# Three more projection units multiplied as eight plain half products, the last attention heads in six steps, the retention gates in a pipeline, and the final norm on three engines

## The chip, the cores and the metric

One core of a Trainium2 chip. The number compared is the device time of one execution in microseconds (us), the median of the runs. A difference of 0.3% (8 us) is about what a measurement of this kernel can tell from no change.

## The reference

Two layers on x of 512 tokens by 2048 (S by D), all in fp32, post-normed: x becomes LayerNorm(2^0.5 · x + branch(x)).

```python
# layer one, "FoX": 16 heads of 128
q, k, v, gate, f = split(x @ fox_w_in)              # 4 x 2048 columns + 16
q, k = rms_norm per head; c = cumsum(log_sigmoid(f + b))
s = q @ k.T * 128**-0.5 + c[query] - c[key]         # causal
y = (softmax(s) @ v) * silu(gate);  branch = y @ fox_w_out
# layer two, retention: 8 heads, q and k of 256, v and gate of 512
q, k, v, gate = split(x @ ret_w_in);  q, k = rotary(q, k)
o = ((q @ k.T) * decay) @ v                         # causal, by chunks
y = group_norm(o) * silu(gate);  branch = y @ ret_w_out
```

## The kernel before, in words

**Products.** fp32 operands are split into a high and a low part (`w_h`, `w_l`: an ACT copy, L288, and a DVE subtraction, L289), and each product is three matmuls (high by high, low by high, high by low; L293, L294, L295). The projections are cut into *units*: 16 narrow ones (n0 to n15; 256-column matmuls; queries and keys of two attention heads or of one retention head) and 18 wide ones (w0 to w17; 512 columns; values and gates, and the two output projections, w4, w5 and w14 to w17). A unit is a 2x2 block product. A `Unit` computes it as seven half products (Strassen's scheme): besides the four input blocks it needs four sums of them (`s1` to `s4`) and sums of weights, made block by block on DVE (L494, L498). A `Plain` takes the input blocks `a11`, `a12`, `a21`, `a22` and the weights as they are, in eight half products, and no sums. Each half product is 48 matmuls in four *blocks* of twelve (wide) or two of 24 (narrow); each loads 512 KB of weights on SP's queue. Before, n0, w4 and n8 are `Plain`, the rest `Unit`s.

**Order.** A class `Order` writes out the instruction streams in program order. A *slot* is one block's matmuls; behind it go steps of waiting *tasks* (a generator's code up to its next `yield need(...)`) as far as rings of buffers are free and the running debt of DVE and ACT allows. Where a block cannot go on for want of a buffer or input (`require`), the tasks' steps are written one behind the other with no block between them: a *clump*. Engines run their streams in order. The units' order is n0, w0, n1, w1, n2, n3, w2, n4, n5, w3, n6, n7, w4, w5, half of n8, half of w6, the rest of both, then n9, w7, n10, w8, ..., n15, w13, w14 to w17.

**Around the change.** After each of n0 to n7 a `Pair` of heads is normed (`normed`) and attends (`head`): scores (`scores`, PE), addition of the query's decay on ACT (`c_tok`, L1031), running minimum on DVE, exponential, scaling by the reciprocal sum (ACT), transposes, product with the values (L1058), gating. The result `y`, and its negative `ny`, go by DMAs to DRAM (`y_s`, where the DMA sums them to `s1` to `s4`) and come back for w4 and w5 (`y_raw`). Then the first norm (`to_columns`) turns z into the input blocks of layer two. In layer two `attend` (rotary on DVE, `rope`; split to `qk_h` on ACT) and `retain` (product `inner` by v, group norm, gates) belong to each head. At `retain`'s end four gate tiles (`p` or `gate`) are scaled by `gn_r` (ACT, L1517), transposed (PE, L1521), and evicted as `y` and `ny` (ACT, L1528, L1529); `gate_done` behind the second frees buffer `k0`, which the next wide unit takes for its kept product (`keep`, ACT, L358). Last, w16 and w17 add into z (L1223), and `store` norms a block of 128 tokens with two DVE instructions for each 512 columns (L1609, L1610).

Of the kernel before, what the change touches and what calls it, by code (L numbers as in the profile page):

```python
# [17 lines left out]
P = 128  # L18
D = 2048
# [24 lines left out]
def blocks_of(n, *groups):  # L44

    def of(g):
# [13 lines left out]
EACH = [[(k, n, c, m) for k in (1, 2) for c in range(2) for n in range(2)] for m in range(2)]  # L60

HELD = ([(1, 0, c, m) for c in range(4) for m in range(2)] + [(1, 1, c, 0) for c in range(4)]
        + [(2, 0, c, m) for c in range(4) for m in range(2)] + [(2, 1, c, 0) for c in range(4)]
# [9 lines left out]
RINGS = dict(mmp=2, tmp=4, st=3, q=4, **{t: 1 for t in "k0 k1 k2 in0 in1 g0 g1 g2 d0 b0 b1 b2 f2 f6 f7 f8".split()})  # L73
# [156 lines left out]
def trunk(ctx: ExitStack, tc: tile.TileContext, xq, x, fb_f, columns, wf_in, narrow, wide, ln_g, ln_b, rot, decay,  # L230
          out):
    nc = tc.nc
    pool = ctx.enter_context(tc.tile_pool(name="sb", bufs=1))
# [33 lines left out]

    cols = pool.tile([P, 2 + 2 * KT], F32, name="cols")
# [31 lines left out]
    def new_form(name):  # L300
        forms[name] = [pool.tile([P, 8, 256], F32R, name=name, tag=t) for t in HOME[name]]
        ready[name] = set()
# [8 lines left out]
    class Unit:  # L311
# [3 lines left out]
        def __init__(self, w, n, sink, rows=True, u2="k0"):  # L315
            self.w, self.n, self.sink, self.rows, self.u2 = w, n, sink, rows, u2
# [25 lines left out]
        def keep(self, what, bank):  # L342
            n = self.shape[2]
            if self.wide or what == "u2":
                tag = {"p1": "k0", "p2": "k0", "p5": "k1", "u2": "k2"}[what] if self.wide else self.u2
# [67 lines left out]
        def sum_ahead(self):  # L413

            for i in range(2):
                t = pool.tile([P, 2, 2, 512], F32, name="v_sum", tag=HOME["s1"][i])
                for c in range(2):
                    self.summed["p7", 2 * i + c] = t[:, c]
# [25 lines left out]
    class Block:  # L444
# [59 lines left out]
        def split(self):  # L504
# [10 lines left out]
            if u.last and p == "p4":  # L515
                if c % 2 == 0:
                    u.wide_w = [sb8(f"w_{j}", HOME["a12" if c == 0 else "s2"][i], F32R)
                                              for i, j in enumerate("hl")]
# [55 lines left out]
    class Plain:  # L574


        def __init__(self, w, n, sink, tags, rows=True):
            self.w, self.n, self.sink, self.rows, self.tags = w, n, sink, rows, tags
# [6 lines left out]
        def run(self, order, then={}, before={}, ahead={}):  # L585

            for i, b in enumerate(order):
                same = last if i and order[i - 1][:3] == b[:3] else None
                last = PlainBlock(self, *b, same, then.get(i), before.get(i), ahead.get(i))
                o.push(last)  # L590

# [19 lines left out]
    class PlainBlock:  # L611
# [31 lines left out]
        def ready(self):  # L643
            n = self.u.shape[1]
            return ready.get(f"a{self.m + 1}{self.k}", set()).issuperset(range(n * self.c, n * self.c + n))

        def multiply(self):
# [5 lines left out]
            multiply(u, u.bank[at], forms[f"a{self.m + 1}{self.k}"], self.w, self.c, new, u.left[at] == 0)  # L653
# [11 lines left out]
    def new_quarters(m):  # L665
        for q, t in (("11", "f8"), ("12", "f9")) if m == 0 else (("21", "g0"), ("22", "g2")):
# [6 lines left out]
    def combine(rest, plain):  # L673
# [36 lines left out]
        yield need(until=lambda: plain.left[1, 0] == plain.left[1, 1] == 0)  # L710
        new_form("s3")
        for c in range(2):
# [8 lines left out]
           for f in HOME if i == 0 or f != "a21"} for i in range(3)]  # L721
# [7 lines left out]
    def give_forms(i, half, m, at, y, ny, but=()):  # L729

        for f, sign, more in GIVES[half, m] + ((("a21", 1, 0),) if (i, half, m) == (0, 0, 1) else ()):
            if f in but:
                continue
# [3 lines left out]
    def fetch_form(i, name, tags, at=0, to=8):  # L737

        step = 8 if tags[0][0] == "g" else 4
        for c in range(at, to, step):  # L740
            n = min(step, to - c)
            heads = 4 * i if i else c + n + (0 if name in ("a11", "a21", "s3") else 8)
            if i == 0 and name in ("s1", "s2", "s4"):
                heads = FH
            yield need(until=lambda: given[i > 0] >= heads and any(free[t] for t in tags))
            if c == 0:
# [19 lines left out]
    def fetch_while(i, tags):  # L766

        take = lambda *names: lambda: spawn(fetch_forms(i, names, tags), 1)
        return {"p5": take("a11", "s1"), "p6": take("s2"), "p7": take("s4", "s3"), "p4": take("a12", "a22")}
# [34 lines left out]
    def forget():  # L804
# [55 lines left out]
        fox["tok"] = pool.tile([P, ST, FH], F32, name="c_tok")  # L860
        yield need(mmp=1, pe=0.4)
        t = mmp()
        ct = by4(t)
        for s in range(ST):
            nc.tensor.transpose(ct[:, s, :FH], c[:, s * P:(s + 1) * P], ident[:FH, :FH])
        yield need(dve=0.3)
        nc.vector.tensor_scalar(fox["tok"], ct[:, :, :FH], -1.0, None, op0=ALU.mult)
        give("mmp")
# [806 lines left out]
```

## Time and profile before

| | us |
|---|---|
| median of three runs (lowest, highest) | 2608.29 (2603.34, 2611.29) |
| the profiled execution's own time | 2620.05 |
| span of its trace | 2618.3 |
| PE busy | 2372.2 (91%) |
| DVE busy | 1962.9 (75%) |
| ACT busy | 1268.9 (48%) |
| POOL busy | 216.5 (8%) |
| mean granted PE clock | 0.955 |

The span lacks 1.75 us of the execution's own time. PE's busy time counts a matmul at a lower granted clock with its longer duration, so part of the 91% is stretched work.

### The profile page before, as it was taken

The page shows a single profiled execution, that of the slowest core. Times are in us where ns is not written, and L with a number is a line of the kernel's source. Part 1 is how long each engine was busy: PE and PEld are TensorE (multiplying, and loading weights), DVE is VectorE, ACT ScalarE, POOL GpSimd, SP SyncE. Part 2 cuts the span into 40 slices and gives each one's busy share as a digit, 9 for nine tenths or more (in the row PEclk, how much of TensorE's full clock was granted, in tenths as well). Part 3 has the DMA queues.
Part 4 walks back from the last instruction along what each step waited for, and adds up shares of the span by engine and source line. Part 5 has one row for each costly group of instructions (what it writes and reads, how often), then busy time and mean ns, then how long its engine had stood idle before and what let it go on. Part 6 is the DMA issues. An engine that isn't in the chain of part 4 may idle for free.

```text
span 2618.3 us, 34343 instructions
## 1 busy us (share of the span) xinstructions
PE 2372.2 (91%) x12964; PEld 2037.6 (78%) x12964; DVE 1962.9 (75%) x2547; ACT 1268.9 (48%) x1891; POOL 216.5 (8%) x324
## 2 busy tenths in 40 slices
PE   7999999999989797998898999989998999699994
PEld 7788898897887575787787797968797887577783
DVE  4778777777765376597878688868887887678878
ACT  4445566666556443653443445444544454434431
POOL 0000200210110100000010101010101010110001
PEclk9999999999999898998999999989999999899997
DMA  5455665665654586454564747555754667578674
GB/s 203 137 177 159 194 197 159 210 192 148 199 150 139 135 288 189 162 169 140 178 205 149 221 157 200 166 162 188 206 193 142 200 176 250 148 249 261 213 247 148
DMA packets 194966, 484.80 MB, mean 185 GB/s; under 512 B 19040, under 2 KB 71392, under 8 KB 194800
## 3 DMA queue, kind: packets, MB, share of 16 engines
q1 hardware_dynamic: 161712, 404.46, 47.1%
q0 software_dynamic: 33088, 78.14, 12.5%
q8 instruction: 102, 1.67, 0.2%
q14 instruction: 64, 0.52, 0.1%
HBM read 412.76 MB, written 69.76 MB: 184 GB/s over the span
## 4 chain that ended last, share of the span: by engine, by line
PE 28%; DVE 18%; DMA 7%; ACT 4%; issue 3%; SPq 0%; ACTq 0%; DVEq 0%
PE acc L294 8%; PE acc L293 8%; PE acc L295 8%; DVE w_l L289 7%; DMA w_raw<-in_wide 5%; DVE w_q L498 3%; ACT w_h L288 2%; DVE w_raw L494 1%; PE mmp L293 1%; PE mmp L294 1%; PE mmp L295 1%; DMA ln_g<-in_ln_g 1%; DVE rope L1390 1%; DVE s L289 1%; DMA y_raw<-y_a 0%
## 5 line engine op out<-in xcount | busy, mean ns | idle before, releaser
L288 ACT ACTIVATE w_h<-w_q 128x1024 fp32r<-128x1024 f32 x384 | 405.2, 1058 | 472.3 <-DVE w_q L498 262.1
L289 DVE TENSOR_TENSOR w_l<-w_q,w_h 128x1024 fp32r<-128x1024 f32 x384 | 468.7, 1222 | 185.6 <-ACT w_h L288 180.7
L294 PE MATMUL acc<-w_l,s 128*128 128x512 f32 (+1 forms) x1536 | 567.6, 370 | 38.5 <-DVE w_l L289 38.3
L293 PE MATMUL acc<-w_h,s 128*128 128x512 f32 (+1 forms) x1536 | 569.0, 370 | 26.6 <-ACT w_h L288 16.3
L295 PE MATMUL acc<-w_h,s 128*128 128x512 f32 (+1 forms) x1536 | 562.7, 366 | 0.0
L293 PE MATMUL acc<-w_h,a 128*128 128x512 f32 (+1 forms) x1408 | 512.6, 364 | 29.2 <-DVE p L403 10.8
L288 ACT ACTIVATE w_h<-w_raw 128x1024 fp32r<-128x1024 f32 x328 | 345.2, 1056 | 385.2 <-PE acc L295 124.5
L289 DVE TENSOR_TENSOR w_l<-w_raw,w_h 128x1024 fp32r<-128x1024 f32 x328 | 400.2, 1221 | 150.9 <-ACT w_h L288 144.7
L294 PE MATMUL acc<-w_l,a 128*128 128x512 f32 (+1 forms) x1408 | 506.3, 360 | 4.0 <-DVE w_l L289 4.0
L295 PE MATMUL acc<-w_h,a 128*128 128x512 f32 (+1 forms) x1408 | 505.3, 359 | 0.0
L294 PEld LDWEIGHTS acc<-w_l,s 128*128 128x128 f32 x1536 | 297.3, 194 | 96.8 <-DVE w_l L289 53.6
L293 PEld LDWEIGHTS acc<-w_h,s 128*128 128x128 f32 x1536 | 297.5, 194 | 75.7 <-ACT w_h L288 18.9
L498 DVE TENSOR_TENSOR w_q<-w_q,w_raw 128x1024 f32<-128x1024 f32 x280 | 340.1, 1220 | 17.0 <-DMA w_raw<-in_wide 13.9
L295 PEld LDWEIGHTS acc<-w_h,s 128*128 128x128 f32 x1536 | 297.2, 194 | 45.3
L293 PEld LDWEIGHTS acc<-w_h,a 128*128 128x128 f32 x1408 | 271.2, 193 | 68.9 <-issue 13.7
L294 PEld LDWEIGHTS acc<-w_l,a 128*128 128x128 f32 x1408 | 271.5, 193 | 43.2 <-DVE w_l L289 7.5
L295 PEld LDWEIGHTS acc<-w_h,a 128*128 128x128 f32 x1408 | 270.8, 192 | 38.6
L494 DVE TENSOR_TENSOR w_raw<-w_raw 128x1024 f32<-128x1024 f32 x88 | 107.4, 1221 | 75.5 <-DMA w_raw<-in_wide 69.5
L295 PE MATMUL acc<-a,w_l 128*128 128x256 f32 x464 | 133.5, 288 | 3.0 <-DVE w_l L289 3.0
L293 PE MATMUL acc<-a,w_h 128*128 128x256 f32 x464 | 133.7, 288 | 0.5 <-ACT w_h L288 0.5
L294 PE MATMUL acc<-a,w_h 128*128 128x256 f32 x464 | 133.0, 287 | 0.0
L293 PE MATMUL acc<-s,w_h 128*128 128x256 f32 x448 | 127.3, 284 | 2.8 <-ACT p L358 2.8
(207 smaller groups left out, 3007.9 us busy)
## 6 DMA issues: line engine op xcount, KB each, us to landing
w_raw<-in_wide SPq DMA_DIRECT2D x364, 512.0 KB, 4.1
w_raw<-in_narrow SPq DMA_DIRECT2D x164, 512.0 KB, 3.9
w_q<-in_wide SPq DMA_DIRECT2D x68, 512.0 KB, 4.7
w_q<-in_narrow SPq DMA_DIRECT2D x28, 512.0 KB, 5.2
y_raw<-y_s SPq DMA_DIRECT2D x24, 512.0 KB, 6.1
y_s<-ny POOLq DMA_DIRECT2D x48, 256.0 KB, 6.7
y_s<-y POOLq DMA_DIRECT2D x40, 256.0 KB, 5.7
y_raw<-y_a SPq DMA_DIRECT2D x18, 512.0 KB, 5.9
```

Source lines behind the costliest of these rows:

```text
L288: nc.scalar.activation(h, src, AF.Copy)
L289: nc.vector.tensor_sub(l, src, f32(h))
L293: nc.tensor.matmul(ps, a[0], b[0], start=start, stop=False, skip_group_check=True)
L294: nc.tensor.matmul(ps, a[0], b[1], start=False, stop=False, skip_group_check=True)
L295: nc.tensor.matmul(ps, a[1], b[0], start=False, stop=stop, skip_group_check=True)
L494: nc.vector.tensor_add(self.t, self.t, u.lent.pop(("p3", c)))
L498: nc.vector.tensor_add(u.chain[c], u.chain[c], t)
L1390: nc.vector.tensor_mul(a, raw[j], cos[:, None, :].to_broadcast([P, 2, 512]))
```

## The change

1. Forty transposes of the identity `ident` stand at the start of PE's stream.
2. The query's decay `c_tok` and the ACT addition for it are gone, in all 16 heads; the minimum reads the scores from PSUM.
3. n7, w5 and w6 become `Plain`, so six units are (the instruction lists show 96 more 512-column and 48 more 256-column matmuls of `acc`, three half products). n7 reloads x's block 21 (`again`). w5 and w6 go by `EACH_N`, in which each block loads its own 512 KB.
4. With no sums needed in w5, `ny` and the DMAs for `s1` to `s4` of layer one go: 88 on POOL's queue. Heads 12 to 15 are split straight into `a12` and `a22`.
5. Heads 12 to 15 (`quick`) take six steps instead of eight, scale on DVE instead of ACT, have buffers that let two heads overlap, and `HELD` needs heads 14 and 15 three blocks later.
6. `to_columns` is spread over w5's later blocks, beside smaller moves of buffers.
7. `retain`'s gate loop becomes a pipeline: in one step ACT scales tile t, PE transposes t-1, and ACT evicts t-2.
8. w14 keeps its first product in `in0` and a later sum in `in1`, no longer in `k0` and `k2`.
9. The final norm: s0 and s1 together; ACT scales and shifts, DVE multiplies by the gain, POOL adds the bias; for s2 and s3 half of the columns so, half as before. All stores go on SP's queue.

In the retention unit w8 ACT's stream had the scale of the second gate tile behind a rotary split; `qk_h` by `rope` is that split, `p` by `gn_r` the scale, `w_h` the weights:

```order
L288 ACTIVATE w_h<-w_q 128x1024 x3
L288 ACTIVATE qk_h<-rope 128x1024
L288 ACTIVATE w_h<-w_q 128x1024 x3
L1517 ACTIVATE p_11439<-p_11439,gn_r 128x512
L288 ACTIVATE qk_h<-rope 128x1024
L1528 ACTIVATE y<-mmp 128x512
L1529 ACTIVATE ny<-mmp 128x512
L1517 ACTIVATE p_11439<-p_11439,gn_r 128x512
L358 ACTIVATE p_12663<-acc 128x1024
L288 ACTIVATE w_h<-w_q 128x1024
```

The changed kernel has at that place:

```order
L1650 ACTIVATE p_11352<-p_11352,gn_r 128x512
L296 ACTIVATE w_h<-w_q 128x1024
L1650 ACTIVATE p_11352<-p_11352,gn_r 128x512
L296 ACTIVATE w_h<-w_q 128x1024
L1641 ACTIVATE y<-mmp 128x512
L1642 ACTIVATE ny<-mmp 128x512
L1650 ACTIVATE gate<-gate,gn_r 128x512
L296 ACTIVATE w_h<-w_q 128x1024 x2
L366 ACTIVATE p_12565<-acc 128x1024
L296 ACTIVATE w_h<-w_q 128x1024
L366 ACTIVATE p_12586<-acc 128x1024
```

The first two scales now stand one weight split apart; the next `qk_h` by `rope` stands six rows further on.

In w4, PE's stream before has the last heads' steps in a clump: product with the values (`pT,by_head`), transposes of the probabilities (`ident,p`), of gates and of raw queries, with no weight block between:

```order
L1058 MATMUL mmp<-pT,by_head 128x128
L961 MATMUL mmp<-ident,p 128x128 x4
L1068 MATMUL mmp<-ident,by_head 128x128 x4
L961 MATMUL mmp<-ident,p 128x128 x3
L926 MATMUL mmp<-ident,qk_raw 128x128 x4
L961 MATMUL mmp<-ident,p 128x128 x3
L1058 MATMUL mmp<-pT,by_head 128x512
L1058 MATMUL mmp<-pT,by_head 128x384
L1058 MATMUL mmp<-pT,by_head 128x256
L1058 MATMUL mmp<-pT,by_head 128x128
```

The changed kernel, where a head's product with the values stands in w4 (`acc` rows are the unit's blocks):

```order
L301 MATMUL acc<-w_h,a_7708 128x512
L302 MATMUL acc<-w_l,a_7708 128x512
L303 MATMUL acc<-w_h,a_7709 128x512
L1117 MATMUL mmp<-pT,by_head 128x512
L1117 MATMUL mmp<-pT,by_head 128x384
L1117 MATMUL mmp<-pT,by_head 128x256
L1117 MATMUL mmp<-pT,by_head 128x128
L301 MATMUL acc<-w_h,a_7706 128x512
```

Such a product now has a block of twelve `acc` matmuls on either side.

At the end DVE's stream before had pairs of norm instructions behind the statistics of the last blocks:

```order
L1223 TENSOR_TENSOR z<-z,acc 128x512
L1227 BN_STATS ln_st<-z 128x6
L1609 SCALAR_TENSOR_TENSOR z<-z,ln_mv,ln_last 128x512
L1610 SCALAR_TENSOR_TENSOR z<-z,ln_r,ln_last 128x512
L1609 SCALAR_TENSOR_TENSOR z<-z,ln_mv,ln_last 128x512
```

and now has single multiplications of 1024 or 512 columns (L1728; their other parts are on ACT and POOL) among the pairs:

```order
L1749 SCALAR_TENSOR_TENSOR ln_nb<-ln_mv,ln_r 128x1
L1728 TENSOR_TENSOR z<-z,ln_last 128x1024
L1728 TENSOR_TENSOR z<-z,ln_last 128x512
L1756 SCALAR_TENSOR_TENSOR z<-z,ln_mv,ln_last 128x512
L1757 SCALAR_TENSOR_TENSOR z<-z,ln_r,ln_last 128x512
L1319 TENSOR_TENSOR z<-z,acc 128x512
L1323 BN_STATS ln_st<-z 128x6
L1728 TENSOR_TENSOR z<-z,ln_last 128x512
L1336 BN_AGGR ln_mv<-ln_st 128x2
```

The core of the diff:

```diff
+EACH_N = [[(k, n, c, m) for k in (1, 2) for n in range(2) for c in range(4)] for m in range(2)]
 
 HELD = ([(1, 0, c, m) for c in range(4) for m in range(2)] + [(1, 1, c, 0) for c in range(4)]
-        + [(2, 0, c, m) for c in range(4) for m in range(2)] + [(2, 1, c, 0) for c in range(4)]
+        + [(2, n, c, m) for c in range(4) for n, m in ((0, 0), (0, 1), (1, 0))]
         + [(k, 1, c, 1) for k in (1, 2) for c in range(4)])
...
+    take("mmp")
+    warm = psum.tile([P, 512], F32, name="mmp", tag="mmp", bufs=2)
+    for i in range(40):
+        nc.tensor.transpose(warm[:, i % 4 * P:(i % 4 + 1) * P], ident, ident)
+    give("mmp")
...
+            self.quick = i >= 6
...
-                        v = ps[q][:, :n]
-                        nc.scalar.activation(v, v, AF.Identity, bias=fox["tok"][:, q, head:head + 1])
...
+                if t < 3:
+                    yield need(pe=0.6, wait=wait, mmp=1, tmp=1, **least_cost(t))
+                    b = tmp("p")
+                    scores(t)
+                    least(t, b)
+                    wait = 0
+                if 1 <= t < 4:
+                    yield need(act=acts(t - 1, 0.19), dve=0.16 * len(groups[t - 1]), wait=wait)
+                    exps(t - 1)
+                    wait = 0
+                if 2 <= t < 5:
+                    yield need(dve=0.85 * acts(t - 2), wait=wait)
+                    scale(t - 2)
+                    wait = 0
+                if t == 3:
+                    give(d0)
+                if 3 <= t:
+                    yield need(pe=0.6, act=acts(t - 3), wait=wait, mmp=1, **{tag_p: int(t == 3)})
+                    if t == 3:
+                        take(tag_p)
...
+            forms["x" + q], ready["x" + q] = forms["a" + q], set(range(8))
+        ready["a11"] = ready["a21"] = set()
+        home.update(x21=home["s3"], a11=(HOME["s1"][1], HOME["s4"][1]), s1=(HOME["s1"][0], HOME["a11"][0]),
+                    s4=(HOME["s4"][0], HOME["a11"][1]))
+
+        def again():
+
+            for c in range(2):
+                tags = "k2", "k0", "k1"
+                yield need(until=lambda: any(free[t] for t in tags))
+                tag = next(t for t in tags if free[t])
+                take(tag)
+                t = pool.tile([P, 4, 256], F32, name="x_raw", tag=tag)
+                nc.sync.dma_start(t.rearrange("p a b -> p (a b)"), xq[1, 0, c])
+                yield need(dve=1.22, act=1.06, wait=3)
+                if c == 0:
+                    new_form("x21")
+                split_form("x21", t, 4 * c, 4 * c + 4)
+                give(tag)
+            fetch("a11")()
+
...
+
+    Plain(narrow, 7, pairs[7].take, two_banks, kind="x").run(
+        BOTH, then={len(BOTH) // 2 - 1: fetch("a21"), len(BOTH) - 1: late})
...
+    def each_banks():
+        a, b, c = banks
+        banks[:] = b, c, a
+        return {(0, 0): a, (0, 1): b, (1, 0): c, (1, 1): a}
+
+    sink, steps = add_z(1, ALPHA, x_rows, "each")
+    unit = Plain(wide, 5, sink, each_banks)
+    unit.run(EACH_N[0], then={0: lambda s=steps: spawn(s(), 1), 15: lambda: spawn(to_columns(0), 1)})
+    unit.run(EACH_N[1], then={15: lambda: (there.clear(), spawn(to_columns(1), 1))})
...
+            ps = {}
+            for t in range(ST + 2):
+                yield need(act=0.67 * (t < ST) + 1.26 * (t > 1), pe=0.45, tmp=2 * (t > 1), mmp=int(0 < t <= ST))
+                if 0 < t <= ST:
+                    ps[t - 1] = by4(mmp())
+                    for i in range(4):
+                        nc.tensor.transpose(ps[t - 1][:, i], g[t - 1][:, i * P:(i + 1) * P], ident)
+                if t > 1:
+                    q = t - 2
+                    y, ny = by4(tmp("y")), by4(tmp("ny"))
+                    nc.scalar.activation(y, ps[q], AF.Copy)
+                    nc.scalar.activation(ny, ps[q], AF.Copy, scale=-1.0)
+                    give("mmp")
+                    h = self.h % 4
+                    give_forms(1 + self.h // 4, h // 2, q // 2, (slice(None), q % 2, slice(h % 2 * 4, h % 2 * 4 + 4)),
+                               y, ny)
+                    give("tmp", 3)
+                    give("tmp", 3)
+                if t < ST:
+                    nc.scalar.activation(g[t], g[t], AF.Copy, scale=r[t // 2][:, t % 2:t % 2 + 1])
+                if t == 2:
                     self.gate_done()
-                if q == 3:
+                if t == 4:
                     give("k2")
...
+    first.qk_unit.run(EACH[0], then={0: lambda: spawn(combine(True, first.vg_unit), 1)})
+    first.vg_unit.run(EACH_N[0])
     first.qk_unit.run(EACH[1], then={len(EACH[1]) - 1: lambda: spawn(first.attend())})
-    first.vg_unit.run(REST, then={"p4": lambda: spawn(first.retain())})
+    first.vg_unit.run(EACH_N[1], then={len(EACH_N[1]) - 1: lambda: spawn(first.retain())})
...
-    Unit(wide, 14, sink).run(then={"p6": lambda s=steps: spawn(s(), 1)})
+    Unit(wide, 14, sink, u2="in1", p1="in0").run(then={"p6": lambda s=steps: spawn(s(), 1)})
...
+    def by_three(z, cs, r, nb):
+
+        nc.scalar.activation(z, z, AF.Identity, scale=r, bias=nb)
+        nc.vector.tensor_mul(z, z, gb[0][:, cs])
+        nc.gpsimd.tensor_add(z, z, gb[1][:, cs])
...
+        nc.vector.scalar_tensor_tensor(nb, mv[:, :, 0], -1.0, r, op0=ALU.mult, op1=ALU.mult)
+        for s in range(2):
+            for c in (0, 2):
+                yield need(dve=1.22, act=1.06)
+                z, cs = piece(s, c, 1024)
+                by_three(z, cs, r[:, s:s + 1], nb[:, s:s + 1])
+                nc.sync.dma_start(out[s * P:(s + 1) * P, cs], z)
...
-            yield from store(s)
+            z, cs = piece(s, c, 512)
+            if c < 2:
+                by_three(z, cs, r, nb[:, :1])
+            else:
+                nc.vector.scalar_tensor_tensor(z, z, mv[:, 0, 0:1], gb[0][:, cs], op0=ALU.subtract, op1=ALU.mult)
+                nc.vector.scalar_tensor_tensor(z, z, r, gb[1][:, cs], op0=ALU.mult, op1=ALU.add)
+            nc.sync.dma_start(out[s * P:(s + 1) * P, cs], z)
```

367 lines of the change are left out of this document (193 added, 174 removed).

## The prediction

> **What bounds the kernel now.** I read the page first, then the chain of waits, the windows unit by unit, PE's waits, and the timeline at the longest of them.
>
> ```profile
> PE 2372.2 (91%) x12964; PEld 2037.6 (78%) x12964; DVE 1962.9 (75%) x2547; ACT 1268.9 (48%) x1891; POOL 216.5 (8%) x324
> PE 28%; DVE 18%; DMA 7%; ACT 4%; issue 3%; SPq 0%; ACTq 0%; DVEq 0%
> ```
>
> PE sets the time: it is busy 91% of the span. The second line, the chain that ended last, has PE with DVE and DMA behind it, so what is not PE's own work is waiting on the weight splits and on attention's small steps. Next, windows of stretches without a stall, then of the stretches that the change touches. Columns: window, length, busy time (and instructions) of PE, weight load, DVE, ACT and POOL, granted clock, DMA share, GB/s.
>
> ```profile
> 180.00:200.00 20.00, 19.99 (x167) 19.74 (x166) 18.22 (x26) 9.62 (x12) 0.00 (x0) 1.00 0.71 233
> 2472.00:2500.00 28.00, 28.00 (x125) 23.20 (x124) 25.81 (x27) 10.94 (x11) 0.00 (x0) 1.00 0.53 169
> 920.00:960.00 40.00, 39.23 (x173) 32.00 (x172) 32.03 (x31) 19.16 (x19) 0.00 (x0) 1.00 0.79 284
> 9.12:66.40 57.28, 50.29 (x384) 49.50 (x384) 29.72 (x25) 26.05 (x48) 0.00 (x0) 0.96 0.55 196
> 66.40:737.10 670.70, 650.29 (x3953) 572.36 (x3953) 510.49 (x735) 394.99 (x768) 70.15 (x106) 0.99 0.57 176
> 737.10:791.60 54.50, 46.95 (x367) 45.95 (x366) 37.46 (x51) 25.32 (x47) 4.64 (x6) 0.91 0.56 163
> 791.60:938.90 147.30, 124.30 (x538) 97.39 (x537) 71.81 (x141) 77.30 (x169) 16.20 (x20) 0.91 0.57 166
> 938.90:1046.90 108.00, 88.39 (x360) 69.53 (x359) 72.60 (x90) 46.84 (x55) 9.19 (x12) 0.91 0.71 217
> 1046.90:1203.40 156.50, 139.18 (x763) 120.48 (x762) 115.40 (x129) 81.99 (x109) 2.13 (x4) 0.93 0.50 167
> 1203.40:1266.80 63.40, 56.12 (x392) 53.45 (x391) 47.71 (x55) 23.60 (x28) 0.54 (x1) 0.92 0.51 164
> 1266.80:1364.10 97.30, 88.29 (x377) 70.66 (x377) 76.56 (x101) 44.81 (x53) 11.78 (x18) 0.95 0.57 175
> 1364.10:1411.20 47.10, 47.10 (x367) 45.84 (x366) 39.48 (x56) 18.75 (x23) 0.56 (x1) 1.00 0.56 188
> 1411.20:1508.80 97.60, 85.25 (x378) 69.47 (x377) 75.19 (x85) 44.77 (x54) 11.82 (x18) 0.95 0.63 184
> 1556.20:1645.60 89.40, 84.95 (x377) 69.18 (x377) 72.25 (x83) 43.94 (x52) 9.56 (x13) 0.98 0.62 174
> 1692.70:1791.80 99.10, 86.10 (x378) 70.10 (x377) 74.94 (x85) 44.81 (x54) 10.16 (x14) 0.93 0.59 170
> 1839.20:1925.90 86.70, 83.75 (x377) 67.96 (x377) 72.33 (x83) 43.95 (x52) 11.27 (x17) 1.00 0.65 192
> 1973.00:2074.30 101.30, 87.55 (x378) 71.10 (x377) 75.36 (x85) 45.00 (x54) 11.72 (x18) 0.93 0.61 177
> 2215.90:2335.60 119.70, 93.21 (x384) 74.48 (x382) 82.48 (x107) 47.35 (x54) 12.58 (x18) 0.87 0.65 195
> 2335.60:2419.20 83.60, 78.65 (x338) 64.11 (x337) 69.27 (x64) 39.95 (x39) 4.33 (x8) 0.98 0.77 254
> 2587.60:2618.30 30.70, 0.00 (x0) 0.00 (x0) 25.43 (x69) 0.00 (x0) 2.74 (x6) 0.57 0.31 120
> ```
>
> The first two rows price a matmul without a stall: 20.00/167 = .120 us (256 columns) and 28.00/125 = .224 us (512). Half a product more is therefore 48 × .224 = 10.8 us wide, 5.8 us narrow. Row 5 holds the first heads. Rows 6 to 11 are n7, w4, w5, n8 with w6, n9 and w7 (here "layer one's end"); row 12 is n10, where PE never stops; rows 13 to 17 are w8, w9, w10, w11 and w12; then w14, w15 and the end after PE's last matmul. Where length exceeds PE's busy time, PE is idle, and the clock column shows the second loss: under 1.00, the matmuls behind an idle are stretched.
>
> At layer one's end stand 1392 wide matmuls of `acc` (w4 8, the others 7 products of 48), 1056 narrow, and 349 others (counts by the order; their sum, 2797, is that of the rows). The price is 1392 × .224 = 311.8, 1056 × .120 = 126.7, and 349 × .17 (the middle of the two) = 60: 498.5 us of 627.0. So 128.5 us are lost there: by the same arithmetic 9 in n7, 35 in w4, 29 in w5, 28 in n8 and w6, 14 in n9, 15 in w7 (rounded up by one in all).
>
> **The change, part by part.** PE's waits (engine, line, what it waited for; us, times, longest; the first two over the span, the next two at layer one's end) and the timeline at three stalls:
>
> ```profile
> PE mmp L1521 <- ACT p L1517: 47.9, 6, 13.9
> PE acc L294 <- DVE w_l L289: 42.3, 35, 4.8
> PE acc L293 <- ACT u L358: 7.6, 1, 7.6
> PE mmp L293 <- DVE sm L1035: 7.2, 2, 6.6
> ```
>
> ```profile
> 1438.14 1.06 ACT L288 ACTIVATE qk_h<-rope 128x1024 fp32r<-128x1024 f32 x1 [8.06 <-DVE rope L1394]
> 1440.06 0.72 ACT L1517 ACTIVATE p<-p,gn_r 128x512 f32<-128x512 f32 x1
> 1440.83 1.12 PE L1521 MATMUL mmp<-ident,p 128*128 128x128 f32 x4 [9.94 <-ACT p L1517]
> 2247.89 2.01 ACT L288 ACTIVATE s<-y_raw 128x1024 fp32r<-128x1024 f32 x2 [7.52 <-DMA y_raw<-y_s]
> 9.12 0.58 PE L293 MATMUL acc<-w_h,a 128*128 128x256 f32 x1 [9.12 <-ACT w_h L288]
> 13.96 0.41 PE L295 MATMUL acc<-w_h,a 128*128 128x256 f32 x1
> 14.18 0.41 PE L293 MATMUL acc<-w_h,a 128*128 128x256 f32 x1
> ```
>
> *Gates in a pipeline: −34.* In w8 PE stood 9.94 us at the second gate's transposes. Their scale (.72 us) was not slow; it stood on ACT behind a `qk_h` split that itself waited 8.06 us for DVE's rotary. w10 and w12 have the same order; w9 and w11, where the scale comes ahead of the split, do not wait. In the changed order all seven later heads have that second pattern. The three then fall to the mean of the calm two: 97.60 + 99.10 + 101.30 − 3 × (89.40 + 86.70)/2 = 33.9. Bounds: 0, if the next `qk_h` wait merely catches the next thing, and 38, with w11 as the measure. What stands behind the wait on ACT then is the weight splits, which have blocks of cover.
>
> *w14's buffers: −17.* w14 has 36.1 us more than w15. The longest of the gates' waits, 13.9 us, lies in it, where ACT stood 7.52 us for a `y_raw` transfer ahead of the scale. With `in0` and `in1` for the kept products the gate transposes spread over blocks. But w14 still holds the last head's product `inner` by v in one piece, since that is what frees `in0`, and has 46 instructions more on PE than w15 (384 − 338), some 46 × .224 = 10 us. 36 − 10 = 26; I leave 9 for the clump that stays. Bounds 5 and 26.
>
> *Layer one's end: −40.* The three `Plain` units cost 2 × 10.8 + 5.8 = 27.6 us of PE, certainly. What they buy is fewer waits: no sums to be formed from late heads, fewer weight sums on DVE, and head steps spread over blocks. What stays I size from like rows. n7 as a `Plain`: n0's window, 57.28 for 384 × .120 = 46.1, says 11, of which 2 belong to the cold start, so 9, as now. w4, w5 and w6 by w9 and w11, which lose 7.0 and 4.3 by the price above (336 × .224 + 41 or 42 × .17): heads 12 to 15 are heavier than a retention head, so 12, 10 and 10; n8 6 (its rotary is new beside a norm), n9 8, w7 6. Sum 61; 128.5 − 61 − 27.6 = 39.9. Bounds: n10 shows that no wait at all is possible (n7's 9 alone left: 128.5 − 9 − 27.6 = 92), and if every wait stays, 27.6 is simply lost.
> Queues: 88 DMAs less on POOL, 24 more 512 KB loads of wide weights on SP (364 to 388 by the order), and `again`'s two loads of x, which stand on SP's queue behind weights already issued and ahead of others. The loads are hidden as long as the queue runs ahead:
>
> ```profile
> w_raw<-in_wide SPq DMA_DIRECT2D x364, 512.0 KB, 4.1
> L498 DVE TENSOR_TENSOR w_q<-w_q,w_raw 128x1024 f32<-128x1024 f32 x280 | 340.1, 1220 | 17.0 <-DMA w_raw<-in_wide 13.9
> L1031 ACT ACTIVATE mmp<-mmp,c_tok 128x512 f32<-128x512 f32 x16 | 10.5, 654 | 3.3 <-DVE o L1071 2.2 <-PE mmp L295 1.1
> 1.12 0.29 POOL masks.py:199 TENSOR_SCALAR_AFFINE_SELECT ident<-ident 128x128 f32<-128x128 f32 x1
> L1610 DVE SCALAR_TENSOR_TENSOR z<-z,ln_r,ln_last 128x512 f32<-128x512 f32 x16 | 12.0, 752 | 0.6
> 2614.09 0.75 DVE L1610 SCALAR_TENSOR_TENSOR z<-z,ln_r,ln_last 128x512 f32<-128x512 f32 x1
> ```
>
> *The decay's addition: −5.* 64 ACT instructions go, the largest .654 us. It stands in the chain from scores to minimum, but ACT is 48% busy and blocks cover it; the windows before n7 hold only 670.70 − 650.29 = 20.4 us of idle in all, partly other waits. Bounds 0 and 20; I take a quarter, since L1031 itself waits little.
>
> *The start: −2.* The first matmuls follow each other by 14.18 − 13.96 = .22 us instead of .120 until about 14.5, some 25 of them: 2.4 us. The identity is ready at 1.12 + .29. Forty transposes at .28 (1.12/4, taken behind an idle) last 11.3 us, to 12.7, which would hold the first product, ready at 9.12, by 3.6; at half of that once the clock rises they end near 9.5. Bounds +4 and −2.4; I take −2.
> The Trainium skill, "TensorE: Matmul & The Clock Gate", Part 4, says of transposes in PE's transpose mode that the full clock does not engage for them. By that the forty would leave this term at about zero or a little above; the trace before has no long run of transposes to show it.
>
> *The final norm: −5.* PE's last matmul is followed by 30.70 us, of them 25.43 of DVE. The norm's 32 instructions at .75 (24.0 us; a few stand before that end) become 8 at .75, 4 multiplications of 1024 columns at 1.22 (L498's size) and 4 of half that: 13.3. With a round of small factors less (s0 and s1 together) that is −12 at best. POOL gets 4 × 1024 + 4 × 512 = 6144 columns of additions; its nearest row, .29 us for 128 columns, makes 2.3 us for 1024 and 13.9 in all. If they run beside DVE, −12; if an addition and a two-input DVE instruction exclude each other, 13.3 + 13.9 is 3 above 24.0, less 2 for the factors: +1. I take −5, near the middle, because no row is near either.
> The Trainium skill, "SBUF — State Buffer", section "SBUF: two separate sides", says that GpSimd and a VectorE instruction with two SBUF inputs share a port pair as an exclusive lock; by it the upper end holds, and the sum would be 97. No run here shows it.
>
> **Sum.** 34 + 17 + 40 + 5 + 2 + 5 = 103 us off the profiled execution, 2620.05. That stood 11.8 above the median of the runs, 2608.29; taken off the median, it gives 2505.
>
> **Rivals.**
> *Layer one's end keeps its waits.* For it: w4's and w5's waits have many causes (`sm`, `u`, `w_h`), so one cured shows the next; heads 12 to 15 now scale on DVE, and two heads overlap. Against: the sums and 26 weight sums of 1.220 us are gone. The 40 becomes 0 (40 of the 67 us of waits that I remove stay): 2545.
> *The gate wait only moves.* PE's stall was in truth DVE's late rotary; if PE meets it at the `qk_h` products a little further on, 34 becomes 5: 2534. Against: w9 and w11 have the same rotary, and PE busy at 84.95 and 83.75.
> *More than summed.* The clock column, under 1 wherever PE stalls, says that a removed stall also removes stretched matmuls; with layer one's end at its bound (92) and w14 at its own, 2444.
> *Slower: weights run short.* With `EACH_N` a block of twelve matmuls lasts 2.7 us and needs 512 KB; three buffers make 8.1 us, less split 1.06 (ACT) and 1.22 (DVE): a load has 5.8 us from issue to landing, against 4.1 at the median. To cancel 103 us over the 64 blocks of w5 and w6, each must wait 1.6 us: landing at 5.8 + 3 × 1.6 = 10.6 us. At 920 to 960 PE ran at 39.23 of 40 with 284 GB/s, above the 512 KB/2.7 us = 194 GB/s here, so it would need a queue stopped by something else.
> *No effect.* The waits at all places are replaced by like ones, and 2600 to 2616 results.
>
> **How the numbers follow.** Forecast .53 (2480 to 2530); waits kept at layer one's end .15; gate wait moved .13; more than summed .12; weights short .04; no effect .03. The range 2460 to 2550 takes in the first three and half of the fourth; it leaves out about .13, and its ends also hold the sums of smaller bounds (w14 12, final norm 7, start 6). 0.3% is 8 us, about what a measurement of this kernel can tell from no change. Faster .93, same .03, slower .04, from the same cases.
>
> **What would show it.** PE's wait for the gates' scale falls from 47.9 us to under 10, and w8, w10 and w12 take 86 to 91 us each. From n7's start to w7's end about 587 us (627 − 40), with the clock near .95. w14 near 103. After PE's last matmul some 25 us instead of 30.7. PE's instructions rise, while its idle time falls by more than 100 us. I am wrong if w5 and w6 wait for `w_raw`, if the waits for `qk_h` or `sm` grow by tens of us, or if POOL's additions each stretch a DVE instruction beside them.

## The result, and the profile after

The changed kernel takes 2473.11 us in the median (2469.09 to 2477.42, four runs) against 2606.16 (2603.34 to 2611.29): a ratio of 0.9488, 95% interval 0.9464 to 0.9511. The forecast was 2505 in 2460 to 2550. Its profiled execution took 2474.03 us, near its median; that of before stood 12 to 14 us above its own, so the traces differ by 146 us where the medians differ by 133. One of the five executions of a run further down (the one with joint factors) took 11225.13 us, from a cause that nothing here shows, and no reading rests on it.

The page's first line, and the chain that ended last:

```profile
PE 2350.8 (95%) x13144; PEld 2027.2 (82%) x13144; DVE 1909.1 (77%) x2507; ACT 1227.3 (50%) x1794; POOL 153.1 (6%) x224
PE 56%; DVE 22%; DMA 8%; issue 7%; ACT 6%; POOL 0%; ACTq 0%; DVEq 0%; SPq 0%; POOLq 0%
```

PE has 180 instructions more, 27 us of added products among them, and is busy 21 us less: fewer matmuls run stretched behind an idle (the mean granted clock went from .955 to .984). PE's share of the chain went from 28% to 56%. The windows of the same stretches (columns as before): the first heads; n7, w4, w5, n8 with w6, n9, w7; w8, w10, w12; w14, w15; the end. Then two of PE's waits over the span.

```profile
61.00:727.10 666.10, 647.56 (x3948) 569.69 (x3949) 507.86 (x733) 371.29 (x710) 20.64 (x38) 0.99 0.50 164
727.10:786.00 58.90, 56.70 (x448) 55.36 (x447) 31.79 (x73) 26.76 (x65) 1.08 (x2) 0.98 0.42 136
786.00:902.50 116.50, 109.72 (x504) 88.61 (x503) 65.11 (x121) 51.99 (x106) 0.00 (x0) 0.98 0.49 156
902.50:997.70 95.20, 91.98 (x417) 74.67 (x415) 56.54 (x77) 47.23 (x65) 2.15 (x4) 1.00 0.64 215
997.70:1143.80 146.10, 141.89 (x812) 123.20 (x813) 107.47 (x120) 82.67 (x100) 2.13 (x4) 1.00 0.61 204
1143.80:1192.50 48.70, 48.70 (x380) 47.35 (x379) 41.64 (x62) 19.83 (x25) 0.55 (x1) 1.00 0.57 184
1192.50:1278.50 86.00, 83.40 (x378) 68.06 (x378) 73.32 (x86) 45.50 (x55) 11.28 (x17) 1.00 0.68 203
1325.60:1414.10 88.50, 85.25 (x378) 69.10 (x377) 74.09 (x98) 44.54 (x53) 10.69 (x16) 0.98 0.64 189
1595.40:1684.30 88.90, 85.36 (x378) 69.09 (x377) 74.01 (x98) 44.52 (x53) 9.28 (x12) 0.98 0.63 176
1865.20:1952.30 87.10, 83.95 (x379) 67.91 (x378) 73.96 (x98) 44.62 (x53) 10.65 (x16) 1.00 0.63 191
2093.40:2190.20 96.80, 89.23 (x382) 71.33 (x381) 84.83 (x113) 46.13 (x51) 4.76 (x8) 0.96 0.66 215
2190.20:2277.10 86.90, 80.21 (x345) 64.69 (x344) 65.09 (x60) 40.28 (x43) 12.16 (x18) 0.96 0.89 269
2444.80:2472.30 27.50, 0.00 (x0) 0.00 (x0) 23.03 (x43) 3.04 (x4) 13.12 (x7) 0.58 0.34 133
```

```profile
PE mmp L1637 <- ACT p L1650: 1.6, 6, 0.3
PE acc L302 <- DVE w_l L297: 41.5, 33, 7.6
```

The gates' wait went from 47.9 to 1.6 us. Layer one's end now has a clock of .98 to 1.00 where it had .91 to .95, and takes 58.9 + 116.5 + 95.2 + 146.1 + 48.7 + 86.0 = 551.4 us where it took 627.0, with half products of 27 us added. By place (us; the trace of the changed kernel against that of the kernel before):

| | forecast | measured |
|---|---|---|
| start and n0 | −2 | −5.4 |
| first heads (w0 to n6) | −5 | −4.6 |
| layer one's end (n7 to w7) | −40 | −75.6 |
| n10 to n15 with w8 to w12 | −34 | −36.7 |
| w14 | −17 | −22.9 |
| w13, w15, w16, w17 | 0 | +2.4 |
| behind the last matmul | −5 | −3.2 |

Two things make −75.6 look larger than it is as a gain of its own. The trace of before is a long one: from n7 to n9 it took 529.7 us, where two runs below with the same code there (the new gate loop alone, and one declared number alone) took 519.9 and 524.6. And of the 11.3 us of w7, the new gate loop alone brings about 8, as the next section shows.

### The profile page after: what moved, and what is told of

The parts are those of the page before. It is cut to its first block, busy times and chain, and to the rows that moved or that the text cites. A ratio compares the mean times of both kernels' runs of the same rounds, so it can differ in the third digit from the quotient of the medians.

```text
span 2472.3 us, 34350 instructions
## 1 busy us (share of the span) xinstructions
PE 2350.8 (95%) x13144; PEld 2027.2 (82%) x13144; DVE 1909.1 (77%) x2507; ACT 1227.3 (50%) x1794; POOL 153.1 (6%) x224
## 4 chain that ended last, share of the span: by engine, by line
PE 56%; DVE 22%; DMA 8%; issue 7%; ACT 6%; POOL 0%; ACTq 0%; DVEq 0%; SPq 0%; POOLq 0%
PE acc L302 16%; PE acc L301 16%; PE acc L303 16%; DVE w_l L297 9%; DMA w_raw<-in_wide 6%; DVE w_q L506 4%; ACT w_h L296 4%; DVE w_raw L502 2%; PE mmp L301 1%; PE mmp L302 1%; PE mmp L303 1%; PE mmp L1117 1%; PE mmp L972 1%; DVE rsq_t L291 1%; DVE rsq_t L290 1%
## 5 line engine op out<-in xcount | busy, mean ns | idle before, releaser
L301 PE MATMUL acc<-w_h,a 128*128 128x512 f32 (+1 forms) x1616 | 585.8, 362 | 21.0 <-ACT acc L898 5.6
L296 ACT ACTIVATE w_h<-w_raw 128x1024 fp32r<-128x1024 f32 x374 | 394.7, 1057 | 417.8 <-PE acc L303 178.9
L297 DVE TENSOR_TENSOR w_l<-w_raw,w_h 128x1024 fp32r<-128x1024 f32 x374 | 456.5, 1221 | 180.1 <-ACT w_h L296 175.5
L296 ACT ACTIVATE w_h<-w_q 128x1024 fp32r<-128x1024 f32 x344 | 362.6, 1057 | 464.0 <-DVE w_q L506 272.1
L302 PE MATMUL acc<-w_l,a 128*128 128x512 f32 (+1 forms) x1616 | 580.7, 359 | 2.9 <-DVE w_l L297 2.8
L303 PE MATMUL acc<-w_h,a 128*128 128x512 f32 (+1 forms) x1616 | 578.6, 358 | 0.0
L297 DVE TENSOR_TENSOR w_l<-w_q,w_h 128x1024 fp32r<-128x1024 f32 x344 | 420.2, 1222 | 148.1 <-ACT w_h L296 143.7
L302 PE MATMUL acc<-w_l,s 128*128 128x512 f32 (+1 forms) x1344 | 493.1, 367 | 38.8 <-DVE w_l L297 38.7
L301 PE MATMUL acc<-w_h,s 128*128 128x512 f32 (+1 forms) x1344 | 493.6, 367 | 3.3 <-ACT w_h L296 1.9
L303 PE MATMUL acc<-w_h,s 128*128 128x512 f32 (+1 forms) x1344 | 488.7, 364 | 0.0
L301 PEld LDWEIGHTS acc<-w_h,a 128*128 128x128 f32 x1616 | 307.7, 190 | 66.7 <-issue 9.9
L303 PEld LDWEIGHTS acc<-w_h,a 128*128 128x128 f32 x1616 | 307.4, 190 | 44.2
L301 PEld LDWEIGHTS acc<-w_h,s 128*128 128x128 f32 x1344 | 256.6, 191 | 42.7 <-ACT w_h L296 2.3
L303 PEld LDWEIGHTS acc<-w_h,s 128*128 128x128 f32 x1344 | 256.7, 191 | 38.4
```

Source lines behind the costliest of these rows:

```text
L296: nc.scalar.activation(h, src, AF.Copy)
L297: nc.vector.tensor_sub(l, src, f32(h))
L301: nc.tensor.matmul(ps, a[0], b[0], start=start, stop=False, skip_group_check=True)
L302: nc.tensor.matmul(ps, a[0], b[1], start=False, stop=False, skip_group_check=True)
L303: nc.tensor.matmul(ps, a[1], b[0], start=False, stop=stop, skip_group_check=True)
```

## The experiments

Ratios are to the kernel before, with 95% intervals; unit times are from each run's profile. A unit is called calm where the stall at the gates' transposes is absent.

### The gate loop: enough by itself, and not needed

The changed kernel with the old loop, and the kernel before with the new one:

```diff
-            for t in range(ST + 2):     # pipeline
+            for q in range(ST):         # scale, transposes, evictions of one tile
```

> The changed kernel with the gate loop of before alone put back (scale, transposes and evictions of one tile after the other, the buffer given free behind the second). Theory, ACT's order: the scale of the second tile falls behind the rotary split again, PE waits about 10 us at the second transposes in w8, w10 and w12, each of these returns to 97 to 101 us, and the kernel loses 30 to 36 us. Rival, the rotary itself is late: the loop is worth little, under 10 us, since PE meets the same rotary at its next step.

> The kernel before with the pipelined gate loop alone. Theory: w8, w10 and w12 fall to 86 to 91 us, and the kernel gains 30 to 36 us there; w14 gains some 5 to 15 us more, since its clump has the same loop, so 35 to 50 us in all. Rival: 0 to 10 us.

The old loop in the changed kernel costs nothing that can be measured: 2475.88 us, 0.95 (0.9476 to 0.9523). The new loop in the kernel before gives 2571.47, 0.9862 (0.9837 to 0.9888), 34 us. w8 in the changed kernel with the old loop, then in the kernel before with the new one, and the gates' waits of the latter:

```profile
1325.50:1414.80 89.30, 85.73 (x378) 68.92 (x377) 74.10 (x98) 44.27 (x53) 10.73 (x16) 0.98 0.63 186
```

```profile
1389.80:1479.30 89.50, 85.45 (x378) 69.10 (x377) 74.24 (x96) 44.34 (x53) 10.71 (x16) 0.98 0.63 186
```

```profile
PE mmp L1521 <- ACT p L1534: 14.5, 8, 12.8
```

Both are calm, and so are w10 and w12 (88.2 and 89.6 in the one, 90.0 and 89.5 in the other). So my theory (with the old loop these units must go back to 97 to 101) and its rival (the loop is worth little anywhere) each failed in one of the two kernels. ACT's order in the traces says why: in the kernel before with the new loop all four scales of a head stand ahead of the first rotary split, as in the changed kernel, and in the changed kernel with the old loop three do and only the fourth stands behind it. Something else in the change moves the scales too. The gain of 34 us is just under the 35 to 50 expected: w8, w10 and w12 give 29 in the traces, w7 gives 8 that nobody forecast (from 97.3 to 89.4), and w14 only 4.6 (115.1). What is left in the last row, 12.8 us at one place, is w14, whose buffers are the old ones there.

### One declared number

```diff
                 nc.vector.scalar_tensor_tensor(b[:, 0], raw[j][:, 1], -1.0, sin, ...)
-                yield need(dve=1.95, wait=0)
+                yield need(dve=2.1, wait=0)
```

> The kernel before with one number changed: the declared DVE cost of the rotary's second step, 1.95 to 2.1, from which the order is made; no instruction is added or taken away. In ACT's order the first two scales of each head then stand ahead of the rotary split (the calm pattern) for all heads but the last. Theory, the order alone makes the stall: w8, w10 and w12 fall to 88 to 91 us, and the kernel gains 22 to 32 us. Rival, the pipeline itself (one step per tile) is needed: under 8 us.

2610.12 us, 1.0011 (0.9995 to 1.0027): no change. Windows of w8, w10, w12, w9, w13, and two of w13's waits:

```profile
1402.30:1495.10 92.80, 85.14 (x379) 69.01 (x378) 73.97 (x84) 45.41 (x55) 11.25 (x17) 0.98 0.62 185
1680.60:1772.00 91.40, 83.64 (x379) 67.93 (x378) 73.87 (x84) 45.46 (x55) 9.84 (x13) 1.00 0.61 177
1958.40:2051.40 93.00, 85.26 (x379) 69.10 (x378) 73.97 (x84) 45.58 (x55) 11.16 (x17) 0.98 0.61 185
1542.20:1633.50 91.30, 85.11 (x378) 69.02 (x377) 73.92 (x84) 45.37 (x55) 9.80 (x13) 0.98 0.61 176
2098.50:2211.60 113.10, 92.81 (x379) 74.19 (x378) 83.31 (x92) 53.30 (x63) 9.79 (x13) 0.89 0.65 191
```

```profile
PE acc L293 <- ACT u L358: 7.1, 1, 7.1
PE mmp L1521 <- ACT gate L1517: 4.9, 1, 4.9
```

The order did what was said where it changed: w8, w10 and w12 fell by 97.6 + 99.1 + 101.3 − (92.8 + 91.4 + 93.0) = 20.8 us. But w13 grew from 94.2 to 113.1: there the fourth scale now stands behind the second rotary split, and the gate's wait with the kept sum behind it is the old stall in a new place. w9 and w11 grew by 7.4 (91.3 + 92.2 against 89.4 + 86.7). Here the gate wait moved on, as in one of the prediction's rivals, though to a later gate scale and not to the `qk_h` products which that rival names; in the changed kernel it did not.

### Layer one's end: the sums, and the late heads

The kernel before with w5 as `Plain` by `EACH_N`, then with w6 too; and the changed kernel with heads 12 to 15 in eight steps:

```diff
-    Unit(wide, 5, sink).run(EARLY, ...)
+    unit = Plain(wide, 5, sink, each_banks); unit.run(EACH_N[0], ...); unit.run(EACH_N[1], ...)
...
-            self.vg_unit = Unit(wide, 6 + h, self.take_vg)
+                self.vg_unit = Plain(wide, 6, self.first_vg, ...)   # h == 0
```

```diff
-            self.quick = i >= 6
+            self.quick = False
```

> The kernel before with w5 alone as eight plain half products in the order of the changed kernel, the first norm spread over its later blocks; the transfers for the sums are still sent, and not read. PE has 10.8 us more to do. Theory two, the sums were the cause of w5's waits: w5's loss falls from 29.5 to 5 to 10 us, n8 and w6 gain too, and the kernel gains 10 to 25 us. Theory one: w5 waits as before or for the late heads in another place, and the kernel is 0 to 11 us slower.

> The kernel before with w5 and w6 as eight plain half products (and with the first retention head's buffers as w6 then needs them); late heads, n7, gate loop, the declared rotary cost of the other heads and the final norm as before. Beside the run with w5 alone (2589.7) PE has 10.8 us more. Theory, the sums of w6 were the cause of the waits in n8, w6, n9 and w7: n8 and w6 fall from 148 to about 146 in spite of the added work, n9 from 62 to 49, w7 from 97 to 86 to 90, and the kernel gains 15 to 30 us on that run; ACT's order also changes by it (three scales now stand ahead of the first rotary split), so that w8, w10 and w12 fall to 88 to 93 and the whole is 2540 to 2570. Rival, n9 and w7 waited for late heads or the gate loop: n9 stays near 62, and the run is at 2585 or above.

> The changed kernel with heads 12 to 15 in the eight steps of before (scale on ACT, one head after the other), all else as changed. Theory one, the late heads were the cause of the waits at layer one's end: w4 loses 15 us or more of what it gained (from 116 to 130 or more), the units behind it some 10, and the kernel 25 to 50 us. Theory two, the sums for w5 and w6 were the cause: under 10 us are lost, and w5 to w7 stay as they are.

w5 alone: 2589.71 us, 0.9941 (0.9922 to 0.996). w5 and w6: 2548.76, 0.978 (0.9753 to 0.9807). Heads in eight steps: 2487.64, 0.9539 (0.9515 to 0.9563). With w5 alone, w5, n8 with w6, n9 and w7:

```profile
933.30:1027.80 94.50, 91.75 (x417) 74.68 (x415) 56.55 (x77) 47.15 (x65) 2.17 (x4) 1.00 0.64 217
1027.80:1175.80 148.00, 135.11 (x752) 116.47 (x753) 116.21 (x126) 76.15 (x94) 2.13 (x4) 0.95 0.54 182
1175.80:1237.60 61.80, 54.13 (x391) 51.26 (x390) 47.59 (x55) 23.73 (x28) 0.54 (x1) 0.94 0.52 169
1237.60:1334.50 96.90, 86.79 (x378) 69.83 (x377) 76.58 (x101) 44.89 (x53) 11.76 (x18) 0.96 0.58 175
```

With w6 as well, n8 with w6, n9, w7, and w8:

```profile
1026.90:1173.40 146.50, 141.90 (x813) 123.14 (x814) 107.53 (x120) 82.66 (x100) 2.13 (x4) 1.00 0.60 203
1173.40:1222.10 48.70, 48.70 (x380) 47.36 (x379) 41.72 (x62) 19.86 (x25) 0.54 (x1) 1.00 0.57 184
1222.10:1312.80 90.70, 85.26 (x378) 68.91 (x377) 73.53 (x86) 44.75 (x55) 11.27 (x17) 0.98 0.64 192
1359.90:1449.50 89.60, 85.50 (x378) 69.08 (x377) 74.05 (x98) 44.08 (x53) 10.71 (x16) 0.98 0.62 186
```

With slow heads, w4:

```profile
787.20:919.00 131.80, 118.31 (x518) 93.20 (x517) 65.66 (x126) 61.79 (x131) 0.00 (x0) 0.95 0.44 140
```

The half products pay for themselves: w5 goes from 108.0 (104.9 and 106.0 in two other traces with the old w5) to 94.5 with a product more. n8 and w6 go from 148.0 to 146.5 with theirs, at a clock of 1.00, and n9 falls from 61.8 to 48.7, in which PE is busy throughout. This was the theory of the sums. In w5 DVE's busy time fell from 72.60 to 56.55 us. That n9, whose own instructions are the same, waits no more because it comes upon no backlog of DVE is argued from this, not shown. The w6 edit also moved the gates' scales (three ahead of the first split in each head), so that w8 is calm without the new loop (89.6), and w10 and w12 fall to 89.4 and 92.0; with w5 alone the three still take 98 to 101. This is the second sufficient cause. Which detail of it moves them, the first head's buffers or its timing, stays open.

The late heads' six steps are worth 15 us, all in w4 (131.8 against 116.5), and 13 to 15 in the medians, not the 25 to 50 of theory one; the units behind stay as they are. Of w4's 30.8 us another half is thus from elsewhere. It is not `HELD`:

```diff
-        + [(2, n, c, m) for c in range(4) for n, m in ((0, 0), (0, 1), (1, 0))]
+        + [(2, 0, c, m) for c in range(4) for m in range(2)] + [(2, 1, c, 0) for c in range(4)]
```

> The changed kernel with w4's order of blocks of before, in which heads 14 and 15 are needed three blocks earlier. Theory, w4's clump had two halves, the steps of the late heads and the early need: w4 goes from 117 to 122 to 128 us. Rival, the six steps alone took the clump away: w4 stays under 120.

2472.48 us, 0.948 (0.9457 to 0.9503), w4 at 113.4: the later need for heads 14 and 15 brings nothing. Two parts of the change are left for the other half, and no run has either alone: n7 as `Plain` (with its reload, and heads 12 and 13 beginning earlier, in n7), and the end of `ny` and of the 88 DMAs for the sums, which the runs with w5 and w6 still send. Which of them it is stays open.

### The decay's addition

```diff
+                    nc.scalar.activation(ps[q][:, :n], ps[q][:, :n], AF.Copy)
                     nc.vector.tensor_sub(cb[:, n - P:n], cb[:, n - P:n], causal)
```

> The changed kernel with an ACT copy of the scores in place ahead of each minimum, as much ACT work as the decay's addition took (64 instructions, 31.5 us of ACT); no number changes by it, and its cost is not declared to the order. Theory, it stands in the chain that frees the score buffer: the stretch of n0 to n6 grows by 3 to 8 us, w4 by 2 to 6. Rival, blocks cover it: under 2 us in all.

2485.36 us in one run. w0 to n6 took 670.10 us; in the other runs of the changed kernel, without the copy, the same stretch took 663.2 to 666.1 (the second row is the run with the bias on DVE):

```profile
62.60:732.70 670.10, 648.23 (x3948) 569.79 (x3949) 508.22 (x733) 386.48 (x758) 20.63 (x38) 0.99 0.50 163
```

```profile
62.00:725.60 663.60, 645.85 (x3949) 568.06 (x3950) 507.97 (x733) 371.56 (x710) 20.69 (x38) 0.99 0.50 165
```

So it costs 4 to 7 us there, as estimated, and nothing clear in w4 (118.3 against 116.5 to 118.2 in runs without it that have the same order of blocks). The traces of the kernel before and its variants, with the addition, took 667.0 to 670.7 us in that stretch, which fits. One run cannot place the rest of the 12 us by which it stands above the changed kernel.

### w14's buffers

```diff
-    Unit(wide, 14, sink, u2="in1", p1="in0")
+    Unit(wide, 14, sink, u2="k2", p1="k0")
```

> The changed kernel with w14's kept products in the buffers of before, which the last head's gates free. Theory, the buffers: w14 goes from 96.8 to 112 to 118 us, the kernel loses 15 to 20. Rival, the pipelined gates or the freer DMA queue did it: w14 stays under 102 us.

2490.97 us, 0.954 (0.9515 to 0.9565): 18 us in the medians, 8.6 between the two traces, of which that of this run was its fastest execution. w14, w15, and w14's longest wait:

```profile
2094.50:2206.60 112.10, 93.13 (x390) 74.75 (x389) 85.56 (x113) 50.16 (x58) 12.58 (x18) 0.91 0.69 209
2206.60:2289.20 82.60, 78.38 (x338) 63.95 (x337) 69.17 (x64) 39.95 (x39) 4.33 (x8) 0.98 0.79 257
```

```profile
PE mmp L1637 <- ACT p L1650: 11.1, 2, 9.7
```

The buffers bring 15 of w14's 23 us, and w15 gives 4 of them back (82.6 with the old ones, 86.9 with the new). With the new buffers the loop is not needed here either: the changed kernel with the old loop has w14 at 97.3.

### The end, and the start

The bias on DVE; then also the factors of the last two token blocks in one; and the forty transposes left out:

```diff
-        nc.gpsimd.tensor_add(z, z, gb[1][:, cs])
+        nc.vector.tensor_add(z, z, gb[1][:, cs])
```

```diff
-    def last_stores(s):                       # s2 and s3 apart, half of the pieces as before
+    def last_stores():                        # ln_factors(2, 3); all pieces by ACT, DVE and DVE
```

```diff
-    for i in range(40):
-        nc.tensor.transpose(warm[:, i % 4 * P:(i % 4 + 1) * P], ident, ident)
```

> The changed kernel with the final norm's additions of the bias on DVE instead of POOL; ACT's part stays. Theory, POOL's additions and DVE's two-input instructions exclude each other: DVE's instructions go back to .75 and .68 us, the 13.9 us or so of POOL become 7.6 us on DVE, and the stretch behind the last matmul falls from 27.5 us by 2 to 6. Rival, they run beside each other: it grows by 4 to 8 us.

> The changed kernel with the final norm's bias on DVE, and the factors of the last two token blocks worked out together, behind the pieces of the first two; all pieces by ACT, DVE and DVE. Theory, DVE's own work sets the end: sixteen instructions of .68, one round of factors of 2.9 and the end of the statistics: the stretch behind the last matmul falls from 27.5 us (23.2 with the additions on DVE alone) to 18 to 21, and the kernel gains 4 to 8 us on the changed one. Rival, the stores, eight on one queue, set the end: 22 to 25 us.

> The changed kernel without the forty transposes. Theory, they bring the clock up: the first matmuls stand .21 us apart again for about 5 us instead of .12, and n0 is 2 to 3 us longer, less what the first load varies by. Rival, transposes leave the clock where it was: spacing as with them.

The first takes 2472.98 us, 0.9479 (0.9457 to 0.9501), the second 2472.42, 0.9484 (0.9465 to 0.9503): neither differs from the changed kernel. Groups of the changed kernel (POOL's additions, DVE's two norm instructions), then of the one with the bias on DVE, and its end:

```profile
L1729 POOL TENSOR_TENSOR z<-z,ln_last 128x1024 f32<-128x1024 f32 x4 | 10.7, 2676 | 20.1 <-DVE z L1728 20.1
L1757 DVE SCALAR_TENSOR_TENSOR z<-z,ln_r,ln_last 128x512 f32<-128x512 f32 x4 | 5.6, 1412 | 0.1
L1756 DVE SCALAR_TENSOR_TENSOR z<-z,ln_mv,ln_last 128x512 f32<-128x512 f32 x4 | 5.1, 1265 | 0.0
```

```profile
L1757 DVE SCALAR_TENSOR_TENSOR z<-z,ln_r,ln_last 128x512 f32<-128x512 f32 x4 | 3.0, 752 | 0.1
L1756 DVE SCALAR_TENSOR_TENSOR z<-z,ln_mv,ln_last 128x512 f32<-128x512 f32 x4 | 3.0, 744 | 0.0
2444.90:2468.10 23.20, 0.00 (x0) 0.00 (x0) 18.75 (x47) 3.04 (x4) 0.00 (x0) 0.60 0.35 136
```

Beside POOL's additions DVE's instructions take 1412 and 1265 ns instead of 752 and 744. The changed kernel's timeline shows that this is a wait for the end of an addition:

```profile
2443.30 5.56 POOL L1729 TENSOR_TENSOR z<-z,ln_last 128x1024 f32<-128x1024 f32 x2 [1.17 <-DVE z L1728]
2445.13 0.15 DVE L287 TENSOR_SCALAR ln_r<-rsq_t 128x1 int32<-128x1 int32 x1
2445.32 1.26 DVE L290 TENSOR_TENSOR rsq_t<-ln_r 128x1 f32<-128x1 f32 x1
2446.62 2.26 DVE L291 TENSOR_TENSOR rsq_t<-rsq_t,rsq_h 128x1 f32<-128x1 f32 x1
2449.11 0.16 DVE L290 TENSOR_TENSOR rsq_t<-ln_r 128x1 f32<-128x1 f32 x1
```

The two additions ended at 2446.57 and 2448.86. The two-input DVE instructions of one column that fell beside them ended within .02 us of that, at 2446.58 and 2448.88, after 1.26 and 2.26 us instead of .16; the one-input instruction ahead of them (L287) took its .15 us. So the round of small factors alone was held for 3.2 us. Without POOL the end is 23.2 us instead of 27.5, although DVE has more to do. The Trainium skill ("SBUF — State Buffer", section "SBUF: two separate sides") says that a GpSimd instruction that reads SBUF and a DVE instruction with two SBUF inputs share an exclusive lock on a port pair, held by whichever starts first for its whole instruction. These rows agree with it. Little of this reaches the whole time, since w17 grows meanwhile (88.3 us in this run against 86.0). With joint factors the end is 20.0 us, as expected, but w17 grows from 86.0 to 91.0, where PE now waits 3.7 us for DVE's `z`, and the 4 to 8 us expected of the whole did not come:

```profile
2362.40:2453.40 91.00, 83.86 (x337) 66.46 (x335) 69.99 (x86) 34.15 (x33) 11.42 (x16) 0.92 0.73 221
2453.40:2473.40 20.00, 0.02 (x1) 0.00 (x0) 15.14 (x35) 5.75 (x8) 0.00 (x0) 0.55 0.36 143
```

The start: two matmuls of the first product of the kernel without the transposes, then the transposes and two matmuls behind them:

```profile
10.80 0.41 PE L295 MATMUL acc<-w_h,a 128*128 128x256 f32 x1
11.01 0.41 PE L296 MATMUL acc<-w_l,a 128*128 128x256 f32 x1
```

```profile
1.47 6.41 PE L273 MATMUL mmp<-ident 128*128 128x128 f32 x40 [1.47 <-POOL ident masks.py:199]
8.55 0.28 PE L301 MATMUL acc<-w_h,a 128*128 128x256 f32 x1
8.67 0.28 PE L302 MATMUL acc<-w_l,a 128*128 128x256 f32 x1
```

They are .21 us apart without the transposes and .12 with them, and n0 takes 57.0 us against 53.3 to 55.5 (56.7 to 57.3 in the kernel before and its variants, which have no transposes either). The single run without them, 2485.85, holds more than these 2 to 4 us (w12, w13 and w17 are also longer in it), which one run cannot place.

## Why the prediction was right or wrong

- **The sum** was 103 and came to 133 in the medians; the range held, near its lower end. The term that was mis-sized is "what stays, sized from like rows", 61 us at layer one's end. Priced in the same way (1488 × .224 + 1104 × .120 + 347 × .17 = 524.8), 26.6 us stay: n7 2 (9 said), w4 10 (12), w5 4 (10), n8 and w6 6 (16), n9 1 (8), w7 4 (6). I had sized n7 by the cold n0, and in the units behind w4 I had carried present losses forward. The w5 and w6 edits alone took those of w5, n8, w6 and n9 away, and either those or the new gate loop took 7 to 8 of w7's 11; that the sums' DVE and ACT work was the way is argued. The added 27 us of half products were priced rightly.
- **Gates, −34**: right in size and in the stall read from the trace, half right on its remover. The new loop suffices, but in this kernel w6's edit alone would have done. The two gains do not add up. The loop's 8 us in w7 were not forecast.
- **w14, −17**: right within its bounds; the buffers bring 15. The rest of the 23 lies between the kernel before and the changed kernel with the old buffers, and no run splits it; the new loop alone brings 4.6 there.
- **Decay, −5**: right, as far as one run shows. **Start, −2**: 5.4, of which 1.5 is the first weights' earlier arrival (chance: the first product began between 7.6 and 9.2 us in the runs of the changed kernel, and between 6.8 and 9.1 in those of the kernel before and its variants) and the transposes 2 to 4. The Trainium skill ("TensorE: Matmul & The Clock Gate", Part 4) says that the full clock does not engage for the transpose mode. The trace has these forty as MATMUL rows and does not show whether they use that mode. They raised the clock all the same: with nothing else on PE they stand .21 us apart up to 5.2 us and .11 from then on.
- **The end, −5**: 3.2, near the forecast by luck, since −5 was only a middle between two bounds. The mechanism is that of the other bound (+1): DVE and POOL do exclude each other here, and POOL's additions did hold up DVE's instructions, which the prediction named as a sign of being wrong.
- **Rivals**: weights did not run short (w5's window moves 215 GB/s at a clock of 1.00). The time lies between the forecast and "more than summed" (2444), in the direction of that rival: of the 102 us of loss that went at layer one's end, 65 were idle time of PE (83.8 before, 19.0 after) and 37 were stretched matmuls (busy time above the price: 44.7 before, 7.6 after). The gate wait moved on with the declared number alone, in the kernel before, and not in the changed one.

## What to carry to other kernels

A scheme with fewer products can lose to the plain one: price it by the waits in its unit and in the units behind it, not only by its own matmuls. A stall that an order makes can have several sufficient cures, and it can come back one place further on; put each cure back and add each alone before crediting it. An idle engine is no free help if its instructions and those of the engine that it relieves hold each other up.

## What the runs showed of the hardware

A two-input DVE instruction that came upon a running POOL addition ended only behind it, even with one column: 1.26 and 2.26 us instead of .16. A one-input DVE instruction at the same time took its usual .15 us. POOL's addition of 1024 columns took 2.68 us in the mean. Forty fp32 transposes against the identity, from 1.47 to 7.88 us, raised the clock by themselves: they stood .21 us apart up to 5.2 us and .11 from then on. The first product's matmuls then stood .12 us apart from the third one on; without the transposes they stood .21 apart until 12.9 us.
